# Making the first overflowing piece's list, rows and weights ready ahead of the loop that computes it

## The chip, the cores and the metric

The kernel runs on one core of a Trainium2 chip. A core has TensorE (PE) for matmuls and transposes, VectorE (DVE), ScalarE (ACT) and GpSimd (POOL) for everything element by element, and SyncE (SP), which here does little but issue DMAs. DMAs issued by SP go to one hardware queue (q1 in the profile), indirect DMAs issued by POOL to a software queue (q0); both are served by the same 16 DMA engines. The metric is device time in microseconds (us) of one execution, both layers together.

## The reference, cut to what matters

```python
def hier_moe(x, ...):                       # after the attention of each of DEPTH = 2 layers
    t = x.reshape(512, 1024)
    lg = t @ rg_w + rg_b; g_star = argmax(lg, -1)            # 1 of 4 groups
    le = (t . re_w + re_b)[g_star]                           # 8 experts of that group
    top_v, top_i = lax.top_k(le, 2)                          # each token: 2 experts of 32
    gate = p_top * softmax(top_v) at (g_star, top_i), else 0
    for g in range(4):
        h = silu(t @ w_gate[g]) * (t @ w_up[g])              # 1024 -> 256, per expert
        y = y + einsum(h * gate[:, g], w_down[g])            # 256 -> 1024
    return y
x = layer_norm(DEEPNORM_ALPHA * x + hier_moe(x, ...), ln2_g, ln2_b)
```

All is float32. The inputs fix which experts get how many of the 512 tokens.

## The kernel before

Each layer is attention (projection, three kinds of heads, output projection, layer norm) followed by the expert stage. The expert stage gives every one of the 32 experts 64 slots and works on pairs of experts, p = 0 to 15, as a block of 128 rows: a list of the tokens in the slots (one-hot matmuls, `lists`), an indirect gather of the tokens' rows from DRAM by POOL (L1013), transposes to `xg`, gate and up matmuls into bank `S`, silu and product, transposes, down matmuls into bank `o`, one multiply-add by the gate weight on DVE for each half of the columns (L1072), and an indirect scatter of the rows to `y2` in DRAM by POOL (L1073). `y2` has a row for a token's first expert (rows 0 to 511) and one for its second (512 to 1023). The weights of an expert are two units of 1.5 MB (gate and up, then down), loaded on SP's queue (`load_next`, L530) into a ring of 13 units, as soon as matmuls of earlier pairs give units back. This stream runs through the whole stage.

An expert with more than 64 tokens leaves the rest to `overflow()`: a hardware loop (L1166) over `n_items` pieces of up to 64 tokens, with `n_items` read from memory. `pieces()`, at p = 3, makes the table of pieces. In this input layer 0 has none, so the loop's body is jumped over there, and layer 1 has one, so the body runs once. The body goes step by step:

- SP reads the expert's number and loads its two weight units (two DMAs of 1.5 MB, into units of the ring);
- DVE makes the list: 20 small operations (L1173 to L1197), four one-hot blocks (L1200), four matmuls of 4 columns into `T`, a copy and the indices (L1207, L991 to L1000);
- POOL gathers the rows by that list (L1013), PE transposes them into `acc` (L1212), DVE scales and shifts them into `xg` (L1215, L1216), beside it the residual rows (L1036, L1037);
- 16 matmuls into `S`, silu (L1222) and product (L1223), two transposes (L1227), 4 matmuls into `o`, two multiply-adds (L1234, L1235) and a scatter that adds in DRAM (L1236).

The body's end waits for all engines and all DMAs that are under way, so that the next turn, or what follows, starts from a known state. There is no such wait ahead of the first turn.

After the loop SP loads the second-expert half of `y2` as `yt`, four tiles of 128 tokens (the first-expert half, `yf`, was loaded ahead, since no piece adds to it). For each tile `yt += yf` (tile 0 on DVE, the others on POOL, L1300), the layer norm on DVE (statistics L1303, L234 to L237 with one power on POOL, L1306, L1308), and, in layer 0, transposes (L1318) and a split of the result into the two float32r halves `xh`, for the next layer's projection. `warm(10)` gives PE ten bf16 matmuls between the loop and the transposes in layer 0. The next layer's first projection weights `w_in` are loaded by `load_pair`, which takes a raw quarter from DRAM and splits it into a high and a low float32r half (ACT takes the high one, DVE or POOL the low one, L194 to L199); in the program's order this stands ahead of `overflow()`, but is issued only after the last pair's matmuls, multiply-adds and scatter.

The order of the work on each engine is set by the program's order and by `issue_after`; a scheduler moves independent instructions of an engine within that.

Of the kernel before, what the change touches and what calls it, by code (L numbers as in the profile page):

```python
# [7 lines left out]
F32 = mybir.dt.float32  # L8
# [56 lines left out]
def trunk(tc, a, out, dbg=None):  # L65
# [4 lines left out]
    with es:  # L70
# [119 lines left out]
        def load_quarter(w, src, q, n, lo_on="VG"):  # L190
            t, k = w[2 * q]
            r = carve(RAW[0], 768 * (wsp["r"] % 4), [2, n])
            wsp["r"] += 1
            SP.dma_start(r, src[:, 2 * q:2 * q + 2, :])  # L194
            hi, lo = t[:, 0, k:k + 2, :], t[:, 1, k:k + 2, :]
# [52 lines left out]
        for l in range(DEPTH):  # L248
# [760 lines left out]
            def gathered(ri, n=128):  # L1009

                xr = carve(xroom, UNIT + D * (turns["x"] % 2), [D])
                turns["x"] += 1
                G.indirect_dma_start(out=xr[0:n], out_offset=None, in_=xd, in_offset=bass.IndirectOffsetOnAxis(ap=ri[0:n], axis=0),  # L1013
                                     bounds_check=S - 1, oob_is_err=False)
                return xr
# [24 lines left out]
            def next_half(p1):  # L1040
                if p1 in XR:
# [56 lines left out]
            def fetch(p):  # L1098
                if p < NE // 2:
                    XR[p] = gathered(RI[p][0])  # L1100

# [38 lines left out]

            def pieces():
# [20 lines left out]

            def overflow():

                n_items = nc.values_load(eidi[0:1, MAX_ITEMS:MAX_ITEMS + 1], min_val=0, max_val=MAX_ITEMS)
                with tc.For_i(0, n_items) as item:  # L1166
                    er = SP.value_load(eidi[0:1, bass.ds(item, 1)], min_val=0, max_val=NE - 1)
                    w = [unit("T", "w") for _ in range(2)]
                    for u in range(2):
                        SP.dma_start(w[u], a["w_e"][l, bass.ds(er, 1), u].rearrange("o p f -> p (o f)"))  # L1170

                    h16 = small.tile([128, 2, MAX_ITEMS], F32, name="h16", tag="h16", bufs=1)
                    V.tensor_scalar(h16[:, 0], cc("item"), ctr[:, 0:1], None, op0=OP.is_equal)  # L1173
                    V.tensor_tensor(h16[:, 0], h16[:, 0], eid, OP.mult)
                    cur = small.tile([128, 4], F32, name="cur", tag="cur", bufs=1)
                    V.tensor_reduce(out=cur[:, 0:1], in_=h16[:, 0], op=OP.add, axis=AX.X)
                    h32 = small.tile([128, 2, NE], F32, name="h32", tag="h32", bufs=1)
                    V.tensor_scalar(h32[:, 0], cc("exp"), cur[:, 0:1], None, op0=OP.is_equal)

# [206 lines left out]
```

## Time and profile before

| | before |
|---|---|
| median of 3 runs | 1354.07 us (1353.26 to 1357.51) |
| profiled execution: time | 1356.09 us |
| profiled execution: span, first to last instruction | 1354.3 us |
| mean granted TensorE clock | 0.948 |
| busy: PE, DVE, ACT, POOL | 1172.7, 794.8, 424.7, 301.4 us |
| bytes moved by DMA | 302.21 MB |
| body of the loop, layer 1 (first list operation to the loads that follow the loop) | 1290.02 to 1321.01 us |
| end, layer 1 (those loads to the last DVE operation) | 1321.01 to 1351.21 us |

The two boundaries that the change touches are the end of layer 0's expert stage, near 646 us, and that of layer 1, from about 1275 us to the end. In a timeline a row is a run of like instructions: start, time until the last one's end, engine, line, operation, written and read tiles, count. PE's float32 matmuls have two records each in the trace, so that a row says x32 where the program has 16. DMAs are shown by their queue (SPq, POOLq) at issue; the time until they have landed is in the views on DMA.

### The profile page before, as it was taken

The numbers are of one execution on the slowest core, as the hardware profiler recorded it, in microseconds if no ns is written. First come the engines' busy times: TensorE is split into PE (matmuls) and PEld (weight loads), VectorE is DVE, ScalarE is ACT, GpSimd is POOL, SyncE is SP. The second block draws the span as 40 slices with busy tenths as digits, with TensorE's granted clock in tenths as the row PEclk, the third lists the DMA queues.
The fourth block names the chain that finished last, engine by engine and source line by source line (L and its number), as shares of the span: only waits on it lengthen the run. The fifth ranks groups of instructions, "written<-read, shape, count | busy, mean of one in ns | idle before, by whom it ended". The sixth has DMA issues, their size and how long they took to land. (4 is left out here: it accounts for less than half of the span.)

```text
span 1354.3 us, 18414 instructions
## 1 busy us (share of the span) xinstructions
PE 1172.7 (87%) x6708; PEld 819.8 (61%) x6708; DVE 794.8 (59%) x2007; ACT 424.7 (31%) x1019; POOL 301.4 (22%) x310
## 2 busy tenths in 40 slices
PE   6989999999969999777599899999998799988830
PEld 6989986668944444232498899666697343333310
DVE  6599638675355745332768992667635465533336
ACT  3462247574112111111236322857711111111100
POOL 5322431300111211100542434230011121111013
PEclk9999999999979999989699999899999799999975
DMA  6452440005188999999542524200335899999933
GB/s 237 115 182 82 125 171 12 22 15 218 63 366 321 424 422 423 425 407 339 194 145 74 198 75 135 104 23 23 131 135 235 317 422 424 423 425 420 392 138 125
DMA packets 68317, 302.21 MB, mean 223 GB/s; under 512 B 16128, under 2 KB 20736, under 8 KB 52864
## 3 DMA queue, kind: packets, MB, share of 16 engines
q1 hardware_dynamic: 57696, 280.02, 53.6%
q0 software_dynamic: 9376, 16.80, 3.3%
q10 hardware_dynamic: 1152, 4.19, 0.8%
q8 instruction: 54, 0.88, 0.3%
q14 instruction: 39, 0.32, 0.1%
HBM read 282.26 MB, written 36.01 MB: 235 GB/s over the span
## 5 line engine op out<-in xcount | busy, mean ns | idle before, releaser
L97 PE MATMUL acc<-U,xh 128*128 128x384 f32 (+1 forms) x1584 | 297.7, 342 | 17.4 <-ACT U L196 7.2
L97 PE MATMUL S<-w,xg 128*64 128x512 f32 (+1 forms) x968 | 265.4, 601 | 31.0 <-DMA w<-w_e 18.5
L97 PEld LDWEIGHTS acc<-U,xh 128*128 128x128 f32 x1584 | 279.8, 193 | 20.2 <-ACT U L196 7.4
L97 PEld LDWEIGHTS S<-w,xg 128*64 128x64 f32 x968 | 88.4, 140 | 155.1 <-issue 103.0
L97 PE MATMUL o<-w,hT 128*64 128x512 f32 x488 | 124.7, 597 | 8.3 <-DVE hT L92 4.4
L199 POOL TENSOR_TENSOR U<-raw,U 128x768 fp32r<-128x768 f32 (+2 forms) x46 | 92.2, 2010 | 176.1 <-ACT U L196 169.3
L1057 ACT ACTIVATE h<-S 128x256 f32<-128x256 f32 x32 | 12.3, 384 | 357.1 <-PE S L97 357.1
L1058 DVE TENSOR_TENSOR h<-h,S 128x256 f32<-128x256 f32 x32 | 13.4, 420 | 175.2 <-ACT h L1057 175.1
L1013 POOL DMA_INDIRECT xroom<-xd,ri x33 | 40.7, 1232 | 261.2 <-issue 193.3
L196 ACT ACTIVATE U<-raw 128x768 fp32r<-128x768 f32 (+2 forms) x88 | 68.2, 812 | 83.0 <-PE acc L97 42.0
L97 PEld LDWEIGHTS o<-w,hT 128*64 128x64 f32 x488 | 40.8, 136 | 72.0 <-issue 49.9
L199 DVE TENSOR_TENSOR U<-raw,U 128x768 fp32r<-128x768 f32 (+2 forms) x42 | 51.5, 1227 | 42.1 <-ACT U L196 39.5
L1072 DVE SCALAR_TENSOR_TENSOR xroom<-o,rv,xroom 128x512 f32<-128x512 f32 x64 | 47.8, 750 | 42.7 <-PE o L97 39.5
L1073 POOL DMA_INDIRECT y<-xroom,ri x32 | 32.7, 1022 | 170.3 <-DVE xroom L1072 146.5
L1028 ACT ACTIVATE xg<-acc,lv 128x128 f32<-128x128 f32 x128 | 48.1, 456 | 57.1 <-PE acc L1024 55.9
L90 ACT ACTIVATE uc<-T 128x512 f32<-128x512 f32 (+3 forms) x117 | 51.4, 461 | 40.6 <-PE T L297 38.5
L97 PE MATMUL acc<-U,oh 128*128 128x384 f32 (+1 forms) x384 | 63.3, 315 | 0.0
L97 PEld LDWEIGHTS acc<-U,oh 128*128 128x128 f32 x384 | 56.8, 189 | 1.2 <-issue 1.0
L1024 PEld LDWEIGHTS acc<-cst,xroom 128*128 128x128 f32 x256 | 29.7, 149 | 38.2 <-issue 25.9
L1036 DVE TENSOR_TENSOR xroom<-xroom,gb 128x1024 f32<-128x1024 f32 (+1 forms) x33 | 40.2, 1219 | 20.1 <-DMA xroom<-xd,ri 20.0
L403 DVE MATCH_REPLACE8 uc<-m,uc 128x256 f32<-128x256 f32 (+2 forms) x96 | 51.4, 540 | 0.0
L1030 DVE TENSOR_SCALAR xg<-acc,lv 128x128 f32<-128x128 f32 x128 | 43.6, 402 | 12.6 <-PE acc L1024 12.6
(377 smaller groups left out, 2034.5 us busy)
## 6 DMA issues: line engine op xcount, KB each, us to landing
w<-w_e SPq DMA_DIRECT2D x110, 1536.0 KB, 26.0
raw<-w_in SPq DMA_DIRECT2D x64, 384.0 KB, 3.6
xroom<-w_e SPq DMA_DIRECT2D x8, 1536.0 KB, 25.8
w<-w_e SPq DMA_DIRECT2D x24, 512.0 KB, 15.1
y<-uc SPq DMA_DIRECT2D x2, 4096.0 KB, 14.2
raw<-w_o SPq DMA_DIRECT2D x16, 384.0 KB, 3.5
xd<-yn ACTq DMA_DIRECT2D x8, 512.0 KB, 6.8
yf<-y SPq DMA_DIRECT2D x8, 512.0 KB, 11.2
```

What stands on the lines that cost most here:

```text
L90: A.activation(o, i, AF.Copy, scale=1.0 if scale is None else scale)
L97: return PE.matmul(o, l, r, start=start, stop=stop, skip_group_check=True)
L196: A.activation(hi, r, AF.Copy)
L199: e.tensor_tensor(lo, r, hi.bitcast(F32), OP.subtract)
L403: V.match_replace(out=acc_t[i][:, :n], in_to_replace=m8, in_values=acc_t[i][:, :n], imm_value=TAKEN)
L1013: G.indirect_dma_start(out=xr[0:n], out_offset=None, in_=xd, in_offset=bass.IndirectOffsetOnAxis(ap=ri[0:n], axis=0), bounds_check=S - 1, ...
L1024: PE.transpose(t[:, 128 * j:128 * j + 128], xr[:, 128 * k:128 * k + 128], ident)
L1028: A.activation(xg[:, k], o, AF.Identity, scale=lv[:, 0, k, 0:1], bias=lv[:, 0, k, 1:2])
L1030: V.tensor_scalar(xg[:, k], o, lv[:, 0, k, 0:1], lv[:, 0, k, 1:2], op0=OP.mult, op1=OP.add)
L1036: V.tensor_tensor(y[0:n], xr[0:n], gb1[0:n, 0], OP.mult)
L1072: last_on["V"] = V.scalar_tensor_tensor(y[:, c], o[n], rows[1], y[:, c], op0=OP.mult, op1=OP.add)
L1073: return G.indirect_dma_start(out=y2, out_offset=bass.IndirectOffsetOnAxis(ap=rows[2], axis=0), in_=y, in_offset=None, bounds_check=2 * S ...
```

## The change

Five things change.

1. `piece_list()` holds what the body did on DVE and PE for the list. It is called once at p = 5, and `piece_take` copies its result to `RP` (the rows to gather and to scatter to) and `WP` (the gate weights). The first piece's rows are gathered where `fetch(16)` stands.
2. The first piece's weights are loaded at p = 14 into `WX`, two units of the ring, by six indirect DMAs of 128 rows x 1024 on POOL's queue, with indices `widx` that `pieces()` makes. Where there is no piece, all indices are out of bounds.
3. The body starts with the transposes. `piece_list()` for the next piece stands between the transposes and the matmuls into `S`; at the end come `piece_take`, the gather of the next piece's rows, and the two loads of the next piece's weights on SP's queue (after the last piece these are loads of the expert that the table's next entry names, and are not used).
4. The sum of the two halves of `y2` is made on PE: for each tile and half a matmul with the identity matrix of `yf` and one of `yt` into the same bank; in layer 0 tile 3 is added on DVE. `warm(10)` is gone.
5. The raw quarters of the next layer's first `w_in` chunk are loaded ahead of the loop without the `issue_after`; the split comes after the loop, three of its four low halves on DVE (before, two). The second chunk's split now comes after tile 0.

```diff
             def fetch(p):
                 if p < NE // 2:
                     XR[p] = gathered(RI[p][0])
+                elif p == NE // 2:
+                    XR[p] = gathered(RP[:, 0:1], 64)
...
+                V.tensor_scalar(wbase, eid[:, 0:1], NE - 0.5, 2.0 ** 20, op0=OP.is_gt, op1=OP.mult)
...
+            def piece_list():
...
+                V.tensor_scalar(h16[:, 0], cc("item"), ctr[:, 0:1], None, op0=OP.is_equal)
...
+                V.tensor_scalar(ctr, ctr, 1.0, None, op0=OP.add)
+                P = cp.tile([128, NT, 2, CAP], F32R, name="oneh", tag="oneh")
...
+                rv = small.tile([128, 3], F32, name="rv", tag="rv", bufs=8)
+                V.tensor_copy(rv, t[:, 0:3])
+                ri, wr, rs = slot_rows(rv, True)
+                return ri, wr, rs
+
+            def piece_take(r):
+                for d, x in ((RP[:, 0:1], r[0]), (RP[:, 1:2], r[2]), (WP, r[1])):
+                    V.tensor_copy(d, x)
...
+                w, xr = WX, XR.pop(NE // 2)
                 with tc.For_i(0, n_items) as item:
-                    er = SP.value_load(eidi[0:1, bass.ds(item, 1)], min_val=0, max_val=NE - 1)
-                    w = [unit("T", "w") for _ in range(2)]
-                    for u in range(2):
-                        SP.dma_start(w[u], a["w_e"][l, bass.ds(er, 1), u].rearrange("o p f -> p (o f)"))
...
-                    ri, wr, rs = slot_rows(rv, True)
-                    xr = gathered(ri, 64)
+                    er = SP.value_load(eidi[0:1, bass.ds(item + 1, 1)], min_val=0, max_val=NE - 1)
...
                     V.tensor_tensor(xg, xg, gb[1], OP.add)
+                    nxt = piece_list()
                     gu = bank("S")
...
+                    piece_take(nxt)
+                    gather_rows(xr, RP[:, 0:1], 64)
+                    for u in range(2):
+                        SP.dma_start(w[u], a["w_e"][l, bass.ds(er, 1), u].rearrange("o p f -> p (o f)"))
...
                 if p == 3:
                     pieces()
+                if p == 5:
+                    piece_take(piece_list())
+                if p == NE // 2 - 2:
+                    WX = [unit("T", "w") for _ in range(2)]
+                    for u in range(2):
+                        for c in range(3):
+                            G.indirect_dma_start(out=WX[u][:, 1024 * c:1024 * c + 1024], out_offset=None, in_=w_rows,
+                                                 in_offset=bass.IndirectOffsetOnAxis(ap=widx[:, u, c:c + 1], axis=0),
+                                                 bounds_check=DEPTH * NE * 768 - 1, oob_is_err=False)
...
-            with tc.issue_after(last_on["PE"].ins), tc.issue_after(last_on["V"].ins), tc.issue_after(st.ins):
-                if not last:
-                    raw_room()
-                    Wc[l + 1, 0] = load_pair(w_in_src(l + 1, 0), chunks[0][1], "VG")
+            if not last:
+                raw_room()
+                rq = [raw_quarter(w_in_src(l + 1, 0), q, chunks[0][1]) for q in range(4)]
             overflow()
...
-                warm(10)
...
+            zb = {}
+            for i in range(NT - 1):
+                zb[i] = [bank(("acc", "o", "S")[i]) for _ in halves]
+            for ys, f in ((yfs, True), (yts, False)):
+                for i in range(NT - 1):
+                    for t, c in zip(zb[i], halves):
+                        mm(t, ident, ys[i][:, c], f, not f)
             for i in range(NT):
                 z = yts[i]
                 src = [z[:, c] for c in halves]
-                for c in halves if i == 0 else [slice(0, 1024)]:
-                    (V if i == 0 else G).tensor_tensor(z[:, c], z[:, c], yfs[i][:, c], OP.add)
+                if i < NT - 1 or last:
...
+                    src = zb[i]
+                else:
+                    with tc.issue_after(zd.ins):
+                        V.tensor_tensor(z, z, yfs[i], OP.add)
```

On POOL, before, the end of layer 1's expert stage and the loop's head: gathers of rows (`xroom<-xd`), the scatters of pairs (`y<-xroom`), then the count of pieces and the branch.

```order
L1013 DMA xroom<-xd,ri 128x1024
L1073 DMA y_7130<-xroom,ri 1024x1024 x4
L1165 TENSOR_LOAD eidi
L1166 COMPARE_AND_BRANCH
L1166 ISA
L1166 UNCONDITIONAL_BRANCH
```

POOL now, the same place, from the scatter of pair 12 on (`RP` holds the piece's rows, `widx` the rows of its weights).

```order
L1080 DMA y_7216<-xroom,ri 1024x1024
L1021 DMA xroom<-xd,RP 64x1024
L1080 DMA y_7216<-xroom,ri 1024x1024
L1305 DMA w<-w_e,widx 128x1024
L1080 DMA y_7216<-xroom,ri 1024x1024
L1305 DMA w<-w_e,widx 128x1024 x5
L1080 DMA y_7216<-xroom,ri 1024x1024
L1232 TENSOR_LOAD eidi
```

The gather of the piece's rows and the six weight gathers stand ahead of the last scatter, in both layers.

On DVE, before, in the loop's body from the one-hot blocks to the product: what leads to the gather, and what works on the gathered rows (`xroom`, `xg`).

```order
L1200 TENSOR_SCALAR oneh<-cst,pr 128x128 x4
L1207 COPY rv<-T 128x3
L991 TENSOR_SCALAR rr<-rv 128x1
L1000 TENSOR_TENSOR rv<-rv 128x1
L992 SCALAR_TENSOR_TENSOR rr<-rv,rr 128x1
L998 CAST ri<-rr 128x1
L999 TENSOR_SCALAR ri<-rr 128x1
L1036 TENSOR_TENSOR xroom<-xroom,gb 64x1024
L1215 TENSOR_TENSOR xg<-acc,lv 128x512
L1037 TENSOR_TENSOR xroom<-xroom,gb 64x1024
L1216 TENSOR_TENSOR xg<-xg,lv 128x512
```

DVE now, the body's first rows.

```order
L1188 TENSOR_SCALAR h_10800<-cst,ctr 128x16
L1195 TENSOR_TENSOR h_10805<-ends,ni 128x32
L1203 TENSOR_TENSOR pm<-tok 128x128
L1189 TENSOR_TENSOR h_10800<-h_10800,eid 128x16
L1209 CAST rd<-cst 128x4x2
L1043 TENSOR_TENSOR xroom<-xroom,gb 64x1024
L1241 TENSOR_TENSOR xg<-acc,lv 128x512
L1191 TENSOR_REDUCE cur<-h_10800 128x1
L1044 TENSOR_TENSOR xroom<-xroom,gb 64x1024
L1242 TENSOR_TENSOR xg<-xg,lv 128x512
L1193 TENSOR_SCALAR h_10805<-cst,cur 128x32
```

Five small operations and one reduction of the next piece's list stand ahead of `xg`'s last step (L1242); the rest of the list comes behind it.

On PE, before, from the loop's body to the end of the last layer.

```order
L97 MATMUL T<-rd,oneh 128x4 x4
L1212 MATMUL acc<-cst,xroom 128x64 x8
L97 MATMUL S<-w,xg 64x256 x16
L1227 MATMUL T<-cst,h 128x64 x2
L97 MATMUL o<-w,hT 64x512 x4
L1166 REGISTER_ALU
```

PE now, the same stretch up to the sums of tiles 0 to 2.

```order
L1238 MATMUL acc<-cst,xroom 128x64 x8
L97 MATMUL S<-w,xg 64x256 x9
L97 MATMUL T<-rd,oneh 128x4 x3
L97 MATMUL S<-w,xg 64x256 x2
L97 MATMUL T<-rd,oneh 128x4
L97 MATMUL S<-w,xg 64x256 x5
L1254 MATMUL T<-cst,h 128x64 x2
L97 MATMUL o<-w,hT 64x512 x4
L97 MATMUL acc<-yf,cst 128x512 x2
L97 MATMUL o<-yf,cst 128x512 x2
L97 MATMUL S<-yf,cst 128x512 x2
L97 MATMUL acc<-yt,cst 128x512 x2
```

The four list matmuls stand among the sixteen into `S`, and the six sums that take `yf` stand ahead of the first one that takes `yt`.

## Rows read from the trace of the kernel before

**Rows 1.** Chain that ended last, layer 1: start us, us, what

```profile
1299.55 16.66 issue
...
1316.45 3.43 DMA y<-xroom,ri
```

**Rows 2.** Timeline, layer 1: start us, us, engine line op, count, [idle before]

```profile
1272.49 3.65 PE L97 MATMUL o<-w,hT 128*64 128x512 f32 x16 [1.17 <-DVE hT L92]
...
1290.02 0.22 DVE L1173 TENSOR_SCALAR h<-cst,ctr 128x16 f32<-128x16 f32 x1
...
1292.99 1.01 PE L97 MATMUL T<-rd,oneh 128*128 128x4 f32 x4 [4.33 <-DVE oneh L1200]
...
1295.55 0.97 POOL L1013 DMA_INDIRECT xroom<-xd,ri  x1 [4.16 <-DVE ri L999]
...
1302.24 1.22 DVE L1036 TENSOR_TENSOR xroom<-xroom,gb 64x1024 f32<-64x1024 f32 x1 [7.41 <-DMA xroom<-xd,ri]
...
1305.89 5.13 PE L97 MATMUL S<-w,xg 128*64 128x256 f32 x32 [2.51 <-DVE xg L1216]
...
1315.42 0.76 DVE L1235 SCALAR_TENSOR_TENSOR xroom<-o,rv,xroom 64x512 f32<-64x512 f32 x1
...
1321.01 4.41 SPq L1292 DMA_DIRECT2D yt<-y  x5
```

**Rows 3.** DMA, 1276 to 1290 us: issues with count, KB each, median us to landing

```profile
DMA packets 1536, 5.62 MB, mean 402 GB/s; under 512 B 233, under 2 KB 233, under 8 KB 1505
...
w<-w_e SPq DMA_DIRECT2D x2, 1536.0 KB, 13.9
...
y<-xroom,ri POOLq DMA_INDIRECT x1, 7.1
```

**Rows 4.** Line 530, last weight issue of layer 1, and its landing

```profile
L530 SPq DMA_DIRECT2D w<-w_e x1: 328/328/328, 1274.8 to 1274.8; - x1
...
DMA to landing us min/median/max: 11.9/11.9/11.9
```

**Rows 5.** Timeline, end of layer 1

```profile
1331.33 5.08 POOL L1300 TENSOR_TENSOR yt<-yt,yf 128x1024 f32<-128x1024 f32 x2
...
1334.14 3.48 DVE L1308 SCALAR_TENSOR_TENSOR yt<-yt,mv 128x512 f32<-128x512 f32 x2
...
1345.79 0.69 DVE L1303 BATCH_NORM_STATS2 bst<-yt 128x6 f32<-128x512 f32 x1
...
1349.80 1.41 DVE L1308 SCALAR_TENSOR_TENSOR yt<-yt,mv 128x512 f32<-128x512 f32 x2
```

**Rows 6.** Timeline, end of layer 0

```profile
646.55 2.29 SPq L1292 DMA_DIRECT2D yt<-y  x5
...
646.64 4.03 PE L97 MATMUL o<-bfc 128*128 128x512 bf16 x10 [9.69 <-DVE ctr L1161]
...
662.45 1.97 PE L1318 MATMUL T<-cst,yt 128*128 128x128 f32 x8 [11.78 <-DVE yt L1308]
```

**Rows 7.** DMA, 1290 to 1303 us

```profile
y<-xroom,ri POOLq DMA_INDIRECT x1, 9.1
...
xroom<-xd,ri POOLq DMA_INDIRECT x1, 6.7
```

**Rows 8.** DMA, 240 to 330 us, an idle stretch

```profile
w<-w_e SPq DMA_DIRECT2D x2, 1536.0 KB, 7.3
```

**Rows 9.** Timeline, layer 0: two f32 matmuls of 512 columns, then one

```profile
269.69 1.88 PE L97 MATMUL acc<-uc,wq 128*128 128x512 f32 x4
...
271.40 1.02 PE L97 MATMUL acc<-uc,wk 128*128 128x512 f32 x2
```

**Rows 10.** Stretches of layer 0: busy us by engine, granted clock, DMA share, GB/s

```profile
648.00:650.00 2.00, 2.00 (x6) 0.65 (x5) 1.17 (x2) 0.00 (x0) 2.00 (x1) 0.50 0.94 254
...
650.00:652.00 2.00, 0.67 (x3) 0.14 (x1) 1.85 (x3) 0.00 (x0) 0.15 (x1) 0.97 0.84 230
...
662.00:664.00 2.00, 1.55 (x7) 1.55 (x8) 2.00 (x4) 0.40 (x1) 0.00 (x0) 0.50 0.06 25
```

More of the change, by code (lines that the diff above doesn't have):

```diff
@@ L194, in load_quarter @@
             SP.dma_start(r, src[:, 2 * q:2 * q + 2, :])
+            return r
+        def load_quarter(w, src, q, n, lo_on="VG", r=None):
+            t, k = w[2 * q]
+            r = raw_quarter(src, q, n) if r is None else r
             hi, lo = t[:, 0, k:k + 2, :], t[:, 1, k:k + 2, :]
@@ L1040, in next_half @@
             def next_half(p1):
-                if p1 in XR:
+                if p1 in XR and p1 < NE // 2:
                     with tc.issue_after(last_on["h"].ins):
@@ L1189, in overflow @@
-                    V.tensor_tensor(pm[:, 1], pm[:, 1], hb, OP.mult)
-                    pr = small.tile([128, 2, NT], F32, name="pr", tag="pr", bufs=1)
-                    V.tensor_reduce(out=pr, in_=pm, op=OP.add, axis=AX.X)
-                    V.tensor_scalar(pr[:, 0], pr[:, 0], cur[:, 3:4], None, op0=OP.add)
-                    rd = small.tile([128, NT, 4], F32R, name="rd", tag="rd", bufs=1)
-                    V.tensor_copy(rd[:, :, 0::3], cc("row").unsqueeze(2).to_broadcast([128, NT, 2]))
@@ L1195, in overflow @@
-                    V.tensor_copy(rd[:, :, 1], pr[:, 1])
-                    V.tensor_tensor(rd[:, :, 2], pr[:, 1], rd[:, :, 1].bitcast(F32), OP.subtract)
-                    V.tensor_scalar(ctr, ctr, 1.0, None, op0=OP.add)
-                    P = cp.tile([128, NT, 2, CAP], F32R, name="oneh", tag="oneh")
-                    for i in range(NT):
-                        V.tensor_scalar(P[:, i], cc("slot")[:, 0:CAP].unsqueeze(1).to_broadcast([128, 2, CAP]), pr[:, 0, i:i + 1], None, op0=OP.is_equal)
@@ L1202, in overflow @@
-                    two = (slice(0, 64), slice(64, 128))
-                    t = bank("T")
-                    for i in range(NT):
-                        mm(t[:, 0:4], P[:, i].rearrange("p a s -> p (a s)"), rd[:, i], i == 0, i == NT - 1)
-                    rv = small.tile([128, 3], F32, name="rv", tag="rv", bufs=8)
-                    V.tensor_copy(rv, t[:, 0:3])
-                    ri, wr, rs = slot_rows(rv, True)
-                    xr = gathered(ri, 64)
+                    er = SP.value_load(eidi[0:1, bass.ds(item + 1, 1)], min_val=0, max_val=NE - 1)
@@ L1320, in trunk @@
                           t.rearrange("p (k n) -> p k n", k=4))
+                if i == 0:
+                    with tc.issue_after(zd.ins):
+                        Wc[l + 1, 1] = pair_units(chunks[1][1])
+                        for q in range(4):
+                            load_quarter(Wc[l + 1, 1], None, q, chunks[1][1], "VG"[q % 2], rq[q])
             moe.__exit__(None, None, None)
```

78 lines of the change are left out of this document (54 added, 24 removed).

## The prediction

> **What bounds the kernel now.** I read the chain of waits first, for the end of layer 1, since the only turn of the loop's body lies there. It shows 16.66 us of "issue" from 1299.55 (the body's own work, in which no engine has much to do) and then 3.43 us for the scatter that adds [rows 1]. The reader is to see that behind the expert stage nothing runs beside anything: whatever is cut from this chain comes off the time, whatever is added goes on it.
>
> The timeline gives the chain's steps [rows 2]. DVE starts the list at 1290.02, right behind the last pair's multiply-adds; the list's matmuls run at 1292.99; the gather is issued at 1295.55 and its rows are there at 1302.24; the matmuls into S start at 1305.89; the second multiply-add ends at 1316.18; and 1.13 us after the scatter has landed (1316.45 + 3.43 = 1319.88) SP issues the loads of yt, at 1321.01. I call that instant E, and the same in layer 0 E0.
>
> The view of the DMAs gives the other side. From 1276 to 1290 us the engines move 402 GB/s [rows 3], so the stage ends as the weight stream ends: its last piece, issued at 1274.8, lands 11.9 us later, at 1286.7 [rows 4]. Anything put into this stretch is paid for by the last pair.
>
> Last, the tail. Behind E the three additions on POOL take 2.5 us each, and where DVE works beside them its operations are stretched: two of L1308 take 3.48 us, at the very end two take 1.41 [rows 5]. Tile 0 is done at 1337.62, E + 16.6, and all at 1351.21, 13.6 later. In layer 0 E0 is 646.55, and the first transposes come at 662.45, E0 + 15.9; eight take 1.97 us [rows 6].
>
> **The body's head.** The list, the gather and the wait for it go: 1290.02 to 1302.24 is 12.2 us. What comes in its place: six small operations of the next list, the first of which took 0.22 us, so at most 1.3, and I take 0.8, since such operations overlap a little; and the unchanged way from the gathered rows to S (1302.24 to 1305.89, 3.65). So S could start at 1290.02 + 0.8 + 3.65 = 1294.5, 11.4 us earlier [rows 2].
>
> Against it stands that the weights WX (2 x 1536 KB, 3.1 MB) move from behind the last pair into the saturated stretch. No row shows 3.1 MB on POOL's queue there. From below the last pair is not held up at all (0 us), if the queue of SP's older requests is served first; from above by the whole 3.1 MB at 402 GB/s, 7.8 us. What the nearest rows say: a scatter on POOL's queue landed in 7.1 us while SP's loads needed 13.9 [rows 3], so the later queue is not made to wait for the older requests. I take equal shares from the time at which WX is under way. That is after pair 14's matmuls (1272.49 + 3.65 = 1276.14), two multiply-adds (0.76 each), and two issues on POOL, the scatter's, which stands ahead of five of the six gathers, and the first of these (0.97 each, as the body's gather took): 1279.6 [rows 2]. The last pair has 1286.7 - 1279.6 = 7.1 us of transfer left, which at half the rate takes 14.2. So d, its delay, is 7.1 us, and S starts at 1301.6, 4.3 earlier instead of 11.4. WX has then landed, as the same bytes in all have moved as had before.
>
> The Trainium skill, "DMA: Bandwidth & Descriptors", section "Queues, rings and completion order", says that each DMA engine takes turns between the queues that have work, packet by packet. It speaks against this change: by it the delay would be the 7.1 us above, and by a rule of first come, first served it would be nothing. The trace agrees so far as 7.1 us against 13.9 go; no row shows two queues that both have megabytes waiting.
>
> **The body's rest.** S to the end of the second multiply-add took 1316.18 - 1305.89 = 10.3 us; the four list matmuls among those of S add at most their own 1.01 [rows 2]. End at 1312.9, scatter 0.27 later. How long this scatter takes to land is open, since the useless loads of a next piece are now beside it: 3.43 us alone [rows 1], 9.1 behind the weight stream, 6.7 for the gather that ran beside two weight loads [rows 7]. This last is what it will be like; I take 6.7: 1319.9. Copies of the next list (two small operations, 0.3) and exit (1.13): E = 1321.3, a loss of 0.3 us (a gain of 3.0 with 3.43, a loss of 2.7 with 9.1). The second useless load starts when the matmuls into o are done, about 2 us before the scatter, at 1311.3, and takes 7.3 us where nothing else runs [rows 8]: 1318.6. The scatter just hides it; were it to take 9 us, it would set E one us later.
>
> The list at p = 5, pieces()' extra operations and POOL's seven issues lie in the part of the stage that the weight stream bounds; I cost them at nothing. If that cover were gone, the list would cost the 5.5 us that it took here until the gather's issue (1290.02 to 1295.55), per layer.
>
> **The sum of the halves.** Two float32 matmuls of 512 columns take 1.88 us and one 1.02 [rows 9], so each further one adds 0.86 at the full clock, and twice that at half. PE has stood still before E, and in layer 0 the granted clock was still 0.50 from 648 to 650 us, PE having begun with its ten warm matmuls at 646.64, and 0.97 in the two us after that [rows 6, 10]. So the six matmuls of yf take 2 x 1.72 + 4 x 0.86 = 6.9 us from E + 0.1, those of yt's tile 0 1.7 more: E + 8.7. The rest of tile 0's norm, undisturbed by POOL, is what the last tile takes from its first statistics to the end, 5.4 us (1345.79 in the same timeline, to 1351.21): E + 14.2 against 16.6. A gain of 2.4 us; the other tiles keep their 13.6, in which DVE has only its own work.
>
> In layer 0 the same reckoning from 646.6 gives 655.2 for tile 0 and 658.6 for tile 2, behind whose sums the transposes stand on PE; DVE is done with tile 0 at 660.6, with its first half 0.7 sooner. The second four transposes, at the full clock, since PE has worked until just before, end near 661.2; they ended at 664.4 (662.45 + 1.97). A gain of 3.2 us. Bounds: a gain of 5 if yt's halves land sooner than they did, a loss of 4.7 if PE stays at half clock (below). Taking the raw w_in quarters earlier costs nothing: they move 1.5 MB in all, and the exit waits for the last scatter as well.
>
> **Sum.** 0.3 - 2.4 - 3.2 = -5.3 us. The profiled execution took 1356.09 us (span 1354.3), 2.0 above the median of the three runs, 1354.07. 1356.09 - 5.3 = 1350.8, and by the median **1348.8 us**.
>
> **Rivals.**
>
> *A, the forecast:* 1348.8, own range 1345 to 1352 (the scatter's landing from 3.43 to 9.1, and d from 4 to 7.8). Chance 0.41.
>
> *B, the last pair is hardly held up.* Then the engines serve the older requests first, WX lands last, around 1294.5, and S starts near 1296.5 at the latest. E = 1296.5 + 11.3 + 0.3 + 6.7 + 1.4 = 1316.2, a gain of 4.8 instead of a loss of 0.3, with the other two terms 10.4 in all; 1343.7 by the median. For it: many rows of WX are issued late, one per us on POOL. Against it: the 7.1 beside 13.9. Chance 0.24.
>
> *C, the change does not do what it says:* the work taken from the head comes back at the body's end, because the exit waits for all that the body prepares for a piece that does not exist. With the scatter's landing at 9.1 E is 2.7 later, the sums give 2.4 back, and in layer 0 the transposes do not start sooner, since yt lands later than it did: 0.3 slower, 1354.4 (1352.5 to 1357). For it: a scatter in company took twice its time alone and more (7.1 to 9.1 against 3.43). Chance 0.20.
>
> *D, slower: PE sums at half clock.* If PE stays at the 1.2 GHz level through the sums, the six of yf take 10.3 us and six of yt as long. In layer 0 the transposes then wait for tile 2's sums, 646.6 + 20.6 = 667.2, a loss of 4.7; in layer 1 tile 0 is done at E + 0.1 + 10.3 + 3.4 + 5.4 = E + 19.2, a loss of 2.6. With E's loss of 0.3 it is 7.6 slower: 1361.7. It decides once PE needs more than about 10 us for yf and tile 0's yt. For it: PE was at the 1.2 GHz level, granted clock 0.50, in the transposes at 662.45, 12 us after the warm matmuls [rows 10]. Against it: the clock rose within 4 us of the first warm matmul at 646.64 [rows 6, 10], and these sums leave PE as little idle as those did. Chance 0.15.
>
> **How the numbers follow.** What a measurement of this kernel can tell from no change is about 0.3%, 4.1 us: faster is below 1350.0, slower above 1358.1. Faster: 0.26 of A's 0.41, nearly all of B (0.23), some of C (0.04): 0.53. Slower: most of D (0.13) and the upper end of C (0.02): 0.15. The rest, 0.32, is the same. The range of 8 in 10 goes from 1340 (B with the scatter at 3.43) to 1358.5 (C's end and beyond, without D).
>
> **What would show it right or wrong.** In the profile after: the last weight piece of the last pair lands later by 7.1 us (0 is B); the matmuls into S start near 1301.6; the landing of the adding scatter is near 6.7; the first loads of yt come near 1321.3; six matmuls of yf take near 6.9 us; and the first transposes of the layer's end in layer 0 start near 660 and end near 661.2. The forecast is wrong if E moves by more than 3 us, if the sums take over 9 us before tile 0's statistics, or if the middle of the stage, which I cost at nothing, grows.

## The result: 1344.73 us, and where the time went

The changed kernel took 1344.73 us (median of 5 runs, 1342.45 to 1347.68) against 1356.38 us (5 runs, 1353.26 to 1357.51) for the kernel before. The ratio is 0.9916, 95% interval 0.9902 to 0.9929: about 11.4 us less by the ratio (11.65 by the medians), where the forecast was 5.3 less. The profiled execution is the one of 1344.73 us; its span is 1342.9 us, again 11.4 below that of before.

Where the 11.4 us are is read by cutting both spans at the same events. The cuts are the first load of yf (issued between the last two pairs), the end of the last pair's down matmuls, the start of S, its end (silu starts), the end of the second multiply-add, the loads of yt (E), the first store of the output, and the end of the span.

| stretch, us | before | changed |
|---|---|---|
| start to the first load of yf in layer 1 | 1276.7 | 1272.0 |
| A: to the end of the last pair's down matmuls | 11.96 | 15.18 |
| B: to the first matmul into S | 17.23 | 5.47 |
| C: S, with the list's matmuls in it now | 5.18 | 9.40 |
| D: silu to the second multiply-add's end | 5.11 | 5.12 |
| E: to the loads of yt | 4.83 | 6.76 |
| F: to the first store (tile 0 done) | 16.64 | 14.28 |
| G: to the end | 16.65 | 14.68 |
| A to G | 77.60 | 70.89 |

So 6.7 us lie behind the first load of yf in layer 1 and 4.7 ahead of it. The timeline of the changed kernel there, which answers to [rows 2, 5] (columns as there; the S matmuls' 32 records are three rows here, with the list's in between):

```profile
1267.87 3.65 PE L97 MATMUL o<-w,hT 128*64 128x512 f32 x16 [1.17 <-DVE hT L92]
...
1288.38 0.23 DVE L1188 TENSOR_SCALAR h<-cst,ctr 128x16 f32<-128x16 f32 x1 [0.40 <-DVE xroom L1079]
...
1292.66 4.53 PE L97 MATMUL S<-w,xg 128*64 128x256 f32 x18 [4.83 <-DVE xg L1242]
...
1297.12 0.80 PE L97 MATMUL T<-rd,oneh 128*128 128x4 f32 x3
1297.86 1.12 PE L97 MATMUL S<-w,xg 128*64 128x256 f32 x4
1298.90 0.37 PE L97 MATMUL T<-rd,oneh 128*128 128x4 f32 x1
1299.21 2.82 PE L97 MATMUL S<-w,xg 128*64 128x256 f32 x10
...
1306.42 0.76 DVE L1262 SCALAR_TENSOR_TENSOR xroom<-o,WP,xroom 64x512 f32<-64x512 f32 x1
...
1307.45 1.48 POOL L1263 DMA_INDIRECT y<-xroom,RP  x1 [5.49 <-DVE WP L1227]
...
1313.94 3.29 SPq L1331 DMA_DIRECT2D yt<-y  x5
1314.27 3.78 PE L97 MATMUL acc<-yf,cst 128*128 128x512 f32 x4 [8.66 <-issue]
...
1321.85 1.88 PE L97 MATMUL acc<-yt,cst 128*128 128x512 f32 x4
```

The list no longer stands ahead of S, but S took 9.4 us with it instead of 5.13. The granted clock tells why it is that long (stretches of the changed kernel, columns as in [rows 10]: the clock is the third number from the end):

```profile
1292.00:1294.00 2.00, 1.34 (x7) 0.77 (x8) 1.97 (x12) 0.00 (x0) 0.00 (x0) 0.50 0.47 186
...
1296.00:1298.00 2.00, 2.00 (x9) 1.09 (x8) 0.00 (x0) 0.00 (x0) 0.00 (x0) 0.50 0.08 31
...
1300.00:1302.00 2.00, 2.00 (x8) 0.69 (x4) 0.23 (x3) 0.00 (x0) 0.98 (x1) 0.52 0.58 98
1302.00:1304.00 2.00, 0.69 (x5) 0.40 (x6) 0.71 (x2) 0.38 (x1) 0.00 (x0) 1.00 0.78 313
```

PE, after 4.83 us of standing still, ran the whole of S at the 1.2 GHz level and had 2.4 GHz back when S was done. In the kernel before, where S began at 1305.89, the clock came back three us into S:

```profile
1306.00:1308.00 2.00, 2.00 (x10) 1.13 (x12) 0.00 (x0) 0.00 (x0) 0.00 (x0) 0.50 0.00 0
1308.00:1310.00 2.00, 2.00 (x18) 1.18 (x16) 0.00 (x0) 0.00 (x0) 0.00 (x0) 0.78 0.00 0
```

The DMAs of the changed kernel from 1276 to 1290 us answer to [rows 3]. Two queues now share the engines (packets, MB, share of 16 engines' time):

```profile
DMA packets 1661, 5.80 MB, mean 414 GB/s; under 512 B 247, under 2 KB 247, under 8 KB 1659
...
q1 hardware_dynamic: 801, 2.92, 51.7%
q0 software_dynamic: 858, 2.87, 50.6%
...
w<-w_e,widx POOLq DMA_INDIRECT x4, 14.4
```

And the last pair's down matmuls take 6.62 us instead of 3.70. The first row is of the kernel before, the others are of the changed kernel: two of PE's weight loads name the landing of weights (in the bracket at the end) as what they came after, and the granted clock was 0.50 for a part of the time.

```profile
1284.96 3.70 PE L97 MATMUL o<-w,hT 128*64 128x512 f32 x16 [0.52 <-ACT hT L90]
```

```profile
1280.57 6.62 PE L97 MATMUL o<-w,hT 128*64 128x512 f32 x16 [0.80 <-issue]
...
1282.72 0.18 PEld L97 LDWEIGHTS o<-w,hT 128*64 128x64 f32 x1 [0.67 <-DMA w<-w_e]
...
1285.26 0.19 PEld L97 LDWEIGHTS o<-w,hT 128*64 128x64 f32 x2 [0.23 <-DMA w<-w_e]
```

```profile
1282.00:1284.00 2.00, 2.00 (x6) 0.47 (x3) 0.00 (x0) 0.00 (x0) 0.00 (x0) 0.50 1.03 420
```

How much of it is the weights and how much the clock is told by the runs below.

The end of layer 0 answers to [rows 6]. E0 is 0.96 us earlier, the first transposes 2.7. But layer 0's first load of yf was already issued 1.26 us earlier (621.95 against 623.21), and from there to E0 the changed kernel takes 0.3 us more:

```profile
645.59 3.12 SPq L1331 DMA_DIRECT2D yt<-y  x5
645.92 3.78 PE L97 MATMUL acc<-yf,cst 128*128 128x512 f32 x4 [10.24 <-DVE ctr L1173]
...
653.17 1.88 PE L97 MATMUL acc<-yt,cst 128*128 128x512 f32 x4
...
657.33 4.03 POOL L203 TENSOR_TENSOR U<-raw,U 128x768 fp32r<-128x768 f32 x2
...
658.11 3.79 DVE L1366 SCALAR_TENSOR_TENSOR yt<-yt,mv 128x512 f32<-128x512 f32 x2
...
659.75 0.66 PE L1376 MATMUL T<-cst,yt 128*128 128x128 f32 x4 [1.26 <-DVE yt L1366]
...
661.96 0.66 PE L1376 MATMUL T<-cst,yt 128*128 128x128 f32 x4 [1.56 <-DVE yt L1366]
```

The two halves of L1366 take 3.79 us here, as POOL splits w_in beside them, where two took 1.41 alone [rows 5]. So tile 0's last transposes end at 662.62, 1.8 earlier than in the kernel before, and its store is issued at 661.93 against 663.09. Counted from E0 the transposes end 17.03 us later against 17.87, a gain of 0.8; counted from layer 0's first load of yf, 0.5.

### The profile page after: what moved, and what is told of

The parts are those of the page before. It is cut to its first block, busy times and chain, and to the rows that moved or that the text cites. A ratio compares the mean times of both kernels' runs of the same rounds, so it can differ in the third digit from the quotient of the medians.

```text
span 1342.9 us, 18636 instructions
## 1 busy us (share of the span) xinstructions
PE 1201.2 (89%) x6756; PEld 834.8 (62%) x6762; DVE 793.6 (59%) x2088; ACT 425.9 (32%) x1019; POOL 291.4 (22%) x317
## 5 line engine op out<-in xcount | busy, mean ns | idle before, releaser
L97 PE MATMUL S<-w,xg 128*64 128x512 f32 (+1 forms) x968 | 268.4, 605 | 28.8 <-DVE xg L1037 14.9
L97 PEld LDWEIGHTS S<-w,xg 128*64 128x64 f32 x968 | 92.6, 141 | 149.3 <-issue 94.7
L97 PE MATMUL o<-w,hT 128*64 128x512 f32 x488 | 127.8, 603 | 8.3 <-DVE hT L92 3.9
L203 POOL TENSOR_TENSOR U<-raw,U 128x768 fp32r<-128x768 f32 (+2 forms) x45 | 86.7, 1931 | 173.1 <-ACT U L200 165.9
L406 DVE MAX8 m<-uc 128x8 f32<-128x256 f32 (+2 forms) x96 | 49.2, 544 | 0.1
## 6 DMA issues: line engine op xcount, KB each, us to landing
raw<-w_in SPq DMA_DIRECT2D x64, 384.0 KB
raw<-w_o SPq DMA_DIRECT2D x16, 384.0 KB
```

The costliest lines, as they stand in the source:

```text
L97: return PE.matmul(o, l, r, start=start, stop=stop, skip_group_check=True)
L203: e.tensor_tensor(lo, r, hi.bitcast(F32), OP.subtract)
L406: V.max(m8, acc_t[i][:, :n])
```

## The experiments

My theory: what the change gained in layer 1 is B less what A, C and E give back, and F and G; what A gives back is the sharing of the engines, C the list's matmuls with PE at half clock, E the loads that nobody uses. Rivals are named with each run. Each was timed beside the kernel before (its median then: 1354.9 for the rows from "list behind S" to "weights late", 1355.7 for the last two rows and "list in S, warm", 1356.7 for the other four). Between executions of the changed kernel and of runs whose instructions up to there are the same, the way to the first load of yf differs by several us (1272.0 to 1278.6 in these profiles), so the stretches A to G of the profiles are compared as well as the times. All in us:

| run | time, median | ratio to before (95%) | A | B | C | D | E | F | G | A to G |
|---|---|---|---|---|---|---|---|---|---|---|
| changed kernel again | 1346.07 | 0.9917 (0.9896–0.9937) | 15.20 | 5.47 | 9.30 | 5.10 | 7.41 | 13.88 | 14.67 | 71.03 |
| list behind S | 1347.95 | 0.9938 (0.9916–0.996) | 14.69 | 5.47 | 5.52 | 6.24 | 6.18 | 14.85 | 14.67 | 67.62 |
| nothing for a next piece | 1343.37 | 0.9899 (0.988–0.9918) | 14.85 | 4.54 | 5.41 | 5.11 | 4.95 | 14.81 | 14.96 | 64.63 |
| old sums | 1352.72 | 0.9978 (0.9963–0.9992) | 15.05 | 5.47 | 6.43 | 5.11 | 6.86 | 15.87 | 16.54 | 71.33 |
| weights late | 1350.13 | 0.995 (0.9933–0.9967) | 12.23 | 7.56 | 10.44 | 5.11 | 6.12 | 14.93 | 14.68 | 71.07 |
| sums alone | 1353.18 | 0.9977 (0.9962–0.9992) | 13.90 | 15.54 | 5.32 | 5.11 | 4.81 | 14.36 | 14.71 | 73.75 |
| no next weights | 1342.86 | 0.9898 (0.9878–0.9918) | 15.06 | 5.46 | 6.44 | 5.11 | 4.77 | 13.56 | 14.99 | 65.39 |
| list behind S, warm | 1341.57 | 0.989 (0.987–0.991) | 15.12 | 5.47 | 3.72 | 7.84 | 6.13 | 11.79 | 14.71 | 64.78 |
| list in S, warm | 1339.21 | 0.9882 (0.9863–0.99) | 15.11 | 5.47 | 4.41 | 6.55 | 6.26 | 11.80 | 14.65 | 64.25 |
| weights behind up | 1347.01 | 0.9929 (0.991–0.9949) | 13.95 | 5.48 | 7.24 | 5.10 | 7.02 | 14.59 | 14.71 | 68.09 |
| the last two together | 1342.57 | 0.9897 (0.988–0.9914) | 14.69 | 5.50 | 4.41 | 5.11 | 7.01 | 13.52 | 14.65 | 64.89 |

**The list's matmuls behind S.**

```diff
-                    nxt = piece_list()
                     gu = bank("S")
...
+                            s_last = mm(gu[c, 0:FH], xg[:, k], ...)
+                    nxt = piece_list(s_last)          # its four matmuls: issue_after(s_last)
```

> The four list matmuls of the next piece are issued behind the sixteen into S instead of among them; nothing else moves. Theory 1: they break the row of S matmuls while PE is still at half clock, and that keeps it there (granted 0.50 from 1292 to 1300 us in the changed kernel, S and list together 9.4 us; the kernel before reached 0.78 three us into S and needed 5.1). Then S takes 5 to 6 us, and the kernel is 2.5 to 4 us faster than the changed one. Rival: the clock has nothing to do with the list; S keeps some 8 us at half clock, and the run is within 1 us of the changed kernel.

S took 5.5 us in one row, 1.1 came back in D, and A to G is 3.3 us shorter than in the changed kernel. The time is not: 1347.95, with an interval that overlaps that of the changed kernel. What the tail gained, this profile had lost ahead of it. The first load of yf came 6.6 us later. Of this 3.3 us were lost before layer 0's first load of yf (625.24 against 621.95), and from the first store of layer 0's result to layer 1's first gather of rows it needed 386.7 us against 384.0, with the granted clock at 0.93 from 750 to 800 us against 1.00. The first row is this run, the second the changed kernel, whose instructions are the same there:

```profile
750.00:800.00 50.00, 46.53 (x259) 44.95 (x259) 46.21 (x122) 15.00 (x28) 19.64 (x22) 0.93 0.38 130
```

```profile
750.00:800.00 50.00, 45.70 (x273) 43.79 (x271) 49.46 (x131) 12.85 (x23) 21.16 (x24) 1.00 0.34 114
```

**Nothing made ready for a next piece** (list, copies, gather and both loads taken out of the body).

> The body makes nothing ready for a next piece: its list, its gather and its two weight loads are left out, so that the loop is right for one piece only. Theory 1: these cost 4.3 us among the S matmuls and 2.1 us in the scatter's landing (5.48 us against 3.43), so S takes near 5 us, the landing 3.4, and the run is 5 to 6.5 us faster than the changed kernel. Rival: the next piece's work is hidden, and the scatter lands late for a reason of its own; then the run gains 1 us at most.

C is 5.4, E 4.95, A to G 6.3 less than in the changed kernel: what the body does for a piece that does not come costs 6.3 us between these two profiles. B shows 0.9 of it (4.54 against 5.47, the six small operations ahead of S), E 1.8; of the 4.0 in C some 3 are the clock, and the next runs show that it need not stay low there. The medians show 1.4 to 2.7 us of the whole, within their spread.

**The sums of the halves as before**, in the changed kernel (the block from `zb = {}` on put back, with `warm(10)`).

> The sums of the two halves of y2 on DVE and POOL as before, with the ten warm matmuls; the loop is the changed one. Theory 1: the sums on PE are worth 4.2 us in layer 1 (first tile done 14.3 us behind the loads instead of 16.6, the other three in 11.7 instead of 13.6) and 2 to 3 in layer 0, so this run is 6 to 7 us slower than the changed kernel. Rival: only the first tile's 2.4 us per layer come from the sums, the rest from the order in which w_in is split; then it is 3 to 5 us slower, with the later tiles of layer 1 still in 11.7 us.

F + G is 32.4 against 29.0, so the sums are worth 3.5 us in layer 1, both in tile 0 and in the later ones; the time is 6.6 to 8 us longer by the medians (1352.72; the twelve times go from 1347.33 to 1356.28, and the profile is one of 1348.47). Where the other 3 us and more of the medians lie is not shown. C took 6.4 here, in the same loop. That raises the question whether the list holds the clock down, or the clock just differs.

**The first piece's weights behind the last scatter.**

```diff
-                if p == NE // 2 - 2:
+                if p == NE // 2 - 1:
                     WX = [unit("T", "w") for _ in range(2)]
+                    with tc.issue_after(st.ins):
```

> The first piece's weights are gathered behind the last pair's scatter instead of at p = 14. Theory 1: the last pair was held up 3 us by sharing the DMA engines, so its down matmuls take 3.7 us again and end 3 us sooner, but 3.1 MB are then still to come at some 400 GB/s, 7.8 us and more from the first issue, and S starts 3 to 6 us later than in the changed kernel; the time is 1 to 6 us longer. Rival: the last pair was held up by PE's clock (0.50 from 1282 to 1284 us), not by its weights; then its down matmuls still take over 6 us here, and the loss is above 6 us.

A is 12.23, as in the kernel before, and S then waits for its weights (B + C 18.0 against 14.9). So without the gathers at p = 14 the last pair is not held up. PE's clock was 1.00 in that pair here, so this run alone does not tell the weights from the clock. The run with the list behind S does: its clock was 1.00 as well, and its last pair was late all the same (A 14.69), with these waits of PE's weight loads:

```profile
1288.88 0.13 PEld L98 LDWEIGHTS o<-w,hT 128*64 128x64 f32 x1 [0.32 <-DMA w<-w_e]
...
1291.34 0.19 PEld L98 LDWEIGHTS o<-w,hT 128*64 128x64 f32 x2 [1.07 <-DMA w<-w_e]
```

```profile
1290.00:1292.00 2.00, 1.81 (x5) 0.47 (x4) 0.00 (x0) 0.00 (x0) 0.00 (x0) 1.00 1.02 416
```

In the three profiles with gathers at p = 14 and the clock at 1.00 all through the last pair A is 14.69, 14.85 and 15.05 (list behind S, nothing for a next piece, old sums); in the five where the clock fell in it, 15.06 to 15.20. So 2.7 to 3.1 us of A's 3.2 are the weights, and the rival is wrong.

A to G as a whole (71.07) is as long as in the changed kernel, so in layer 1 the later gathers gain nothing and lose nothing. That the time is longer, as expected, comes from something that no expectation named: in layer 0, where these six gathers move no bytes, POOL issues them, one each 1.3 us, behind the last scatter, and E0 came 4 us later behind the first load of yf (27.6 against 23.6).

**The changed kernel once more** (no edit).

> The changed kernel once more, for a second profile and times beside the others. In the run with the old sums, whose loop is the same, S and list took 6.4 us and the granted clock rose three us into S; in the changed kernel's profile it stayed at 0.50 and they took 9.4. Theory 1 (the list's matmuls hold the clock down): 9 us again. Rival (where the clock rises in S differs from execution to execution): anything between 6 and 10 us; then the list itself costs some 1 us, and the list behind S brings about 1 us and no more. Either way the last pair ends 15 us after the first load of yf is issued (15.2, 14.7, 14.9, 15.1 in the four profiles with the weights gathered at p = 14; 12.0 and 12.2 in the two without), and the time is 1343 to 1347.

S and the list took 9.3 us, with the clock at 0.50 throughout, and A 15.2. With the same loop, 6.4 with the old sums and without next weights, 7.2 with the weights behind up. In these the clock rose early in S. Its rows in the run without next weights:

```profile
1296.00:1298.00 2.00, 1.77 (x10) 1.02 (x12) 1.97 (x14) 0.00 (x0) 0.00 (x0) 0.50 0.44 176
1298.00:1300.00 2.00, 2.00 (x13) 1.06 (x9) 0.75 (x4) 0.00 (x0) 0.00 (x0) 0.73 0.22 88
1300.00:1302.00 2.00, 2.00 (x16) 1.33 (x17) 0.69 (x6) 0.00 (x0) 0.00 (x0) 1.00 0.06 23
```

So the list's own part is 0.9 to 1.3 us (6.4 against 5.2 to 5.5), and the other 3 are the clock. That the list holds it down is not shown, nor refuted. In the three shorter ones the clock rose 2.8, 2.9 and 4.6 us into S, before the list's first matmul ran or within 0.1 us of it; in the two long ones it had not risen when that matmul ran, 4.5 us into S. What decides it is open; no profile without a list in S had the long form (5.2 to 5.5 in four), which is too few to tell.

**The sums alone** (the kernel before with the block from `zb = {}` on, without `warm(10)`).

> The kernel before with the sums of the two halves of y2 on PE and no warm matmuls, and nothing else of the change. Theory 1: from the loads of yt to the end of layer 1 it takes 29 to 29.8 us instead of 33.3, in layer 0 at most 1 us is gained, so the run is 4 to 5 us faster than the kernel before. Rival: without the loop's other changes the sums start with PE at half clock and yt is waited for anyway; then it is 0 to 2 us faster.

F and G are the changed kernel's (29.1 against 33.3), so 4.2 us come from the sums in layer 1. The time fell by 3.6 (the profile is one of 1357.58, near the longest of the twelve). In layer 0 the first transposes came 18.3 us behind E0, against 15.9 before and 14.2 in the changed kernel:

```profile
661.27 1.81 POOL L199 TENSOR_TENSOR U<-raw,U 128x768 fp32r<-128x768 f32 x1 [8.84 <-ACT U L196]
663.05 0.57 POOL L236 TENSOR_TENSOR mv<-mv,mhalf 128x1 f32<-128x1 f32 x1
...
666.93 1.97 PE L1332 MATMUL T<-cst,yt 128*128 128x128 f32 x8 [5.67 <-DVE yt L1322]
```

The norm's power stands on POOL behind a split of w_in there. In the changed kernel the second chunk's split comes behind tile 0; without that part the sums lose in layer 0, in this profile, more than half of what they gain in layer 1. The last pair's matmuls also took 5.37 us here, with no gathers beside them, in part with the clock at 0.50: by itself the clock cost that pair 1.7 us. Where the weights are late anyway, little of it is left (0.5 at most, by the profiles named above).

By the medians the loop without the sums gained 2.2 us and the sums without the loop 3.6, but both together 10.7 to 11.7. The stretches A to G are shorter by 6.3, 3.9 and 6.7 us; where the times' other differences lie is open.

**No next weights** (the two loads at the body's end taken out).

> The changed kernel without the two loads of a next piece's weights at the body's end, so that the loop is right for one piece only; list and gather of the next piece stay. Theory 1: these loads are what lengthens the way from the second multiply-add to the loads of yt (4.83 us before, 4.95 without any next-piece work, 6.1 to 6.9 with it), so this way is 5 us and the run some 2 us faster than the changed kernel. Rival: the gather that is under way, and the copy of its list behind the landing, are what lengthens it; then it stays above 6 us and the time does not move.

E is 4.77 us, as in the kernel before. The two loads cost 1.4 to 2.6 us (6.1 to 7.4 with them), the gather and the copies nothing; the median is 1.9 to 3.2 us below the changed kernel's.

**List behind S, and PE kept busy.**

```diff
+                    warm(16)                                  # between the transposes and S
...
+                    with tc.issue_after(o_last.ins):          # behind the matmuls into o
+                        warm(28)
```

> The changed kernel with the list matmuls behind S, and in the loop's body sixteen bf16 matmuls between the transposes and S, and 28 behind the matmuls into o, whose result nobody reads. Both theories agree that PE then has its full clock in S and in the sums: S takes 3.5 to 4.5 us (5.4 to 9.4 without), the six sums of yf 5.3 us instead of 7.6, and the run is 3 to 6 us faster than the changed kernel. If the time behind the loads of yt is set by their landing, the sums' part of it, 2 us, is lost.

S took 3.7 us and F 11.8 instead of 14.3: the sums started at the full clock, and tile 0 was done 2.5 us sooner, so it was PE and not yt's landing that set it. D grew to 7.84: the matmuls into o took 3.60 us, with half the clock in them, and the list now stood ahead of the product on DVE.

**The list behind the twelfth matmul into S, and PE kept busy.**

> As the kernel with the list behind S and the warm matmuls, but the four list matmuls are issued behind the twelfth of the sixteen into S. What was left there: the product waited behind a list that was not ready (7.84 us from silu to the second multiply-add instead of 5.1), since S had become 1.7 us shorter. Expected: S with list 4.5 to 5 us, silu to multiply-add 5.1, so 1.5 to 2 us less than in that run between S's start and the multiply-add, and a time of 1339 to 1341. If the list's rows come too late on DVE here too, S stretches to over 6 us and nothing is gained.

The fastest: 1339.21, ratio 0.9882. C is 4.4 us, a little less than expected; D is not as expected, since the matmuls into o again fell to half clock (3.39 us against 1.94), as the row of 1302 shows.

```profile
1294.00:1296.00 2.00, 1.37 (x14) 0.94 (x16) 1.97 (x11) 0.00 (x0) 0.00 (x0) 1.00 0.50 199
...
1302.00:1304.00 2.00, 2.00 (x7) 0.28 (x4) 0.00 (x0) 0.00 (x0) 0.00 (x0) 0.50 0.42 166
```

In both runs with warm matmuls the first transposes of layer 0, where the body does not run, came 13.2 and 12.7 us behind E0 instead of 14.2, so some 1 us of these two profiles' times is not the body's.

**The weights gathered behind the last pair's up matmuls** (`issue_after` these and pair 14's scatter).

> The changed kernel with the first piece's weights gathered behind the last pair's gate and up matmuls and pair 14's scatter, some 5 us later than in the changed kernel. Theory 1 (the last pair's weights and these gathers share the engines about half and half while both are under way, 3 us of delay at p = 14, none behind the last scatter): the last pair ends 12.5 to 14 us behind the first load of yf instead of 15.1, S starts 5.5 us behind that as before, and its weights are there in time; 1 to 2.5 us faster than the changed kernel. Rival: the weights come too late for S; then S starts or runs 2 us and more later and the time is the changed kernel's or longer, as with the gathers behind the last scatter (1350).

A is 1.2 us shorter and S did not wait, and in layer 0 E0 came 23.7 us behind the first load of yf, so there the earlier place costs nothing. But the time did not move: 1347.01.

**Both together:**

> Both together: the list matmuls behind the twelfth into S, the warm matmuls, and the weights gathered behind the last pair's gate and up matmuls. If both do what is expected of them they add up, as they lie in series: 3 to 5 us from the warm clock, 1.5 to 2 from the list's place, 1 to 2.5 from the weights, 1338 to 1340. If the weights come later than S can now use them, the gain of the third is lost.

They did not add up: A is 14.69, with the clock at 0.50 from 1286 to 1288 us, in the last pair's down matmuls, where the run before had 1.00 and 13.95; and 1342.57 is not below the run without the later gathers (1339.21).

## Why the prediction was right in its sign and short by half

The measured time lies just below the range of rival A (1345 to 1352) and inside the whole range (1340 to 1358.5). By one of its own signs the forecast was wrong: E was to move by no more than 3 us and came 7.1 us sooner, 2.4 of it in A to E and 4.7 ahead of the first load of yf.

- *The head* (right). S would start 5.8 us behind the last pair's end (1294.5 against 1288.66, the pair's delay apart); it was 5.47 in every kernel with this loop but the one whose weights came late. This is the gain of the change, 11.8 us.
- *d, the last pair's delay* (mechanism right, size wrong). 7.1 us forecast, 3.2 measured (A). The gathers were under way when forecast (1275.0, 3.0 us behind the first load of yf; forecast 2.9), and the queues shared the engines. The step that failed is the doubling of all the 7.1 us that were left: the last weights landed only 10.3 us later (1285.3), not 14.2. Up to the landing SP's queue moved 2.40 MB, less than the 2.85 that 402 GB/s make in 7.1 us (0.27 of them were pair 14's scatter), and it got more than half of the engines' time. The first two rows are of the kernel before from 1279.6 to 1286.7 us, the others of the changed kernel from 1275.0 to 1285.3 (packets, MB, share):

```profile
q1 hardware_dynamic: 712, 2.58, 92.7%
q0 software_dynamic: 144, 0.27, 10.0%
```

```profile
q1 hardware_dynamic: 659, 2.40, 58.0%
q0 software_dynamic: 561, 1.83, 44.2%
```

2.40 MB at half of 402 GB/s would have been 11.9 us; at the 233 GB/s that the queue got they were 10.3. One reading behind the equal shares was wrong, too: the 13.9 us of [rows 3] are those of the loop body's own two loads, issued nine us after the scatter that landed in 7.1. What bears on the question is that this scatter was issued 2.4 us after the last weights (1274.8) and had landed 2.3 us before them. The conclusion is the same. The kernel before:

```profile
1277.25 0.97 POOL L1073 DMA_INDIRECT y<-xroom,ri  x1 [11.41 <-DVE xroom L1072]
...
1286.28 0.97 SPq L1170 DMA_DIRECT2D w<-w_e  x2
```

- *The list in S* (wrong). 1.0 us forecast, 4.2 in the two profiles of the changed kernel, of which about 1 is the list and 3 the clock, which stayed at 0.50. The term that failed is the 10.3 us from S to the second multiply-add, taken over as they were: in them the clock rose three us into S, and I had not asked whether it still would.
- *The scatter* (right in kind, too long): 6.7 us of landing forecast, 5.48 measured, and the run without the two loads shows that they are the cause.
- *Tile 0 of layer 1* (the number right, in part by luck): 14.2 us behind E forecast (its terms add up to 14.1), 14.28 measured. The sums were done 9.8 us behind E, not 8.7, as the first three of the six matmuls of yf ran at half clock; but the statistics of the first half began before the second half was summed, which gave 0.9 us back. *The later tiles* (wrong): no change forecast, 2.0 us gained. Each one's norm waits for a power on POOL, which took 0.55 us here and 0.99 before, three times one after another: 1.3 of the 2.0. It is not POOL's additions that lengthened it, as they had ended at 1336.41. What differs is DVE's multiply-add beside it, which before took its input from the tile `yt` and now takes it from the bank into which PE summed. Every power of this norm in both kernels goes by that: 0.98 to 1.02 us beside a multiply-add that reads `yt` alone, 0.55 to 0.57 beside one that reads a bank, or beside none. The first two rows are of the changed kernel, the next two of the kernel before; the last two are of the changed kernel again, of the one tile (layer 0, tile 3) that is still summed in `yt`:

```profile
1330.04 0.74 DVE L1364 SCALAR_TENSOR_TENSOR yt<-o,mv,yt 128x512 f32<-128x512 f32 x1
1330.21 0.55 POOL L240 TENSOR_TENSOR mv<-mv,mhalf 128x1 f32<-128x1 f32 x1 [4.18 <-DVE mv L239]
```

```profile
1340.05 0.73 DVE L1306 SCALAR_TENSOR_TENSOR yt<-yt,mv 128x512 f32<-128x512 f32 x1
1340.21 0.99 POOL L236 TENSOR_TENSOR mv<-mv,mhalf 128x1 f32<-128x1 f32 x1 [3.80 <-DVE mv L235]
```

```profile
680.74 0.74 DVE L1364 SCALAR_TENSOR_TENSOR yt<-yt,mv 128x512 f32<-128x512 f32 x1
680.90 0.99 POOL L240 TENSOR_TENSOR mv<-mv,mhalf 128x1 f32<-128x1 f32 x1 [10.33 <-DVE mv L239]
```

- *Layer 0* (wrong: 3.2 forecast, 0.8 measured from E0). The transposes started where forecast (659.75) only because E0 came 0.96 us sooner, which the forecast did not have. What it left out is the splits on POOL, beside which the last two multiply-adds took 3.79 us and not 1.41. From the first store to layer 1's first gather the profile had 2.1 us less (384.0 against 386.1); as runs with the same instructions there needed 383.9 to 387.5, that is not assured.
- *The middle of the stage* (nothing forecast): from layer 1's first gather to the first load of yf 226.0 to 227.2 us in all kernels with the list ahead, 227.5 and 227.9 in the two without. The list at p = 5 costs nothing there; what the 1 us less comes from was not tried.

So of the rivals D is refuted: the clock rose during the sums. B, at 1343.7, came nearest in time, but by luck, as the last pair was held up after all. C's mechanism was there in part, 1.9 us more at the body's end (E) and 4.2 in C, but the head's 11.8 outweighed it. Against the forecast, d gave 3.9 us more, E 1.6, the later tiles 2.0 and the way to the first load of yf 1.5 (4.7 where 3.2 was forecast for layer 0), and C took 3.2: 5.8 of the 6.1 us between forecast and measurement; the head's 0.3 is the rest. The 4.7 are not layer 0's sums, which gave 0.8 at most. What is assured of the whole gain is the 6.7 us in A to G (70.9 and 71.0 in two profiles against 77.6) and what little layer 0's end gives; the other 4 us lie in stretches whose instructions the change hardly touches and which differ by as much between profiles. The medians show them both times (11.7 and 10.7 us less in all), and their cause is open.

## What to carry to other kernels

Preparing the first turn of a loop ahead of it took the latency in front of the first turn off the path, here 11.8 us, at a price of 3.2 us for the work before, with whose loads its own then shared the engines. A loop that runs once also pays for preparing the turn that does not come: here some 2 us for loads that nobody uses, 1 for the list and 1 ahead of S. Where a chain of small steps has PE waiting, count its matmuls at half clock, or give it something to do: forty-four matmuls whose result nobody reads, with the list's matmuls moved, took 6 to 7 us off this tail, although they left the matmuls into o at half clock. When a small operation stands in a chain, look at what another engine does beside it: here a power on POOL took 0.99 us beside a DVE operation that read a tile, and 0.55 beside one that read a bank.

## What the runs showed that I had not expected

- One loop with the same instructions took 6.4 or 9.3 us for S, by whether the granted clock rose three us into it or only at its end. What decides it was not found.
- In profiles of identical instructions the attention of layer 1 differed by up to 3.6 us, with the granted clock of one stretch of 50 us between 0.93 and 1.00. Gains below that have to be read in the tail, not in one run's time.
- Indirect gathers with all rows out of bounds still kept POOL busy 1.0 us each, one every 1.3 us. Issued behind the last scatter they delayed the loads of yt in layer 0 by 4 us; issued ahead of it, by nothing that the runs show (23.6 and 23.7 us from the first load of yf).
